# Seven block products for eight in the second layer's output projection of a hybrid decoder trunk

## The chip, the core and the metric

The kernel runs on one core of a Trainium2 chip. Its time is device microseconds of one execution; where several executions stand together, the median is given with the lowest and the highest. A profile is one execution of its own, recorded by the hardware. In it PE is TensorE (PEld its weight loads), DVE is VectorE, ACT is ScalarE, POOL is GpSimd, and SP is the engine that only issues transfers; SPq, ACTq and so on are what an engine's queue does beside its arithmetic, such as issuing a DMA. "L508" is line 508 of the profiled kernel.

## What is computed

Two decoder layers over 1024 tokens of width 1024 in float32. The reference, cut to what matters here:

```python
def hybrid_layer(x, c_act, ...):
    shift, scale, gate = split(c_act @ w_mod + b_mod, 3)
    h = rms_norm(x, pre_gain) * (1.0 + scale) + shift
    proj = h @ w_in                      # columns of three head groups and their gates
    a_out = sliding_window_attention(aq, ak, av, sinks) * silu(ag)      # 512 columns
    r_out = rms_norm(retention(rq, rk, rv)) * silu(rg)                  # 256 columns
    g_out = rms_norm(gated_linear_attention(...), gla_norm_gain) * silu(gg)  # 256 columns
    y = concatenate([a_out, r_out, g_out], axis=-1) @ w_out             # 1024 x 1024 @ 1024 x 1024
    return x + gate * rms_norm(y, post_gain)
```

The change is in the next-to-last line, for the second layer: the product of the gated mix (1024 tokens by 1024) with w_out (1024 by 1024).

## The kernel before

**Precision.** TensorE multiplies in a reduced float32 form, so every float32 operand is kept as a pair: a rounded high part and the low rest (high part: a cast on ACT or DVE; low part: a subtraction on DVE or POOL). A product is three passes: high by high, low by high, high by low.

**Order of the work.** A planner writes the program. Long rows of matmuls are written out in place (`mult`, `accum`), and every 7 of them `pump` lets waiting jobs (generators such as `gate`, `finish`, the attention blocks) put in their next piece if a table of due times says so. TensorE executes in exactly this order; the other engines' orders come from a scheduler, each engine working through its own queue in order. The table `EN` names the engine of each small operation ("A", "V", "G" are ACT, DVE, POOL; "S" and "A" for a transfer name the queue that issues it). Small tiles come from rings: `t2` (128x512, 14 buffers), `st` (5, weight pieces as they arrive), `smx` (6, softmax tiles), `mx` (2, the mix of one token tile, high and low), `mm` (3 accumulators of 512 columns in PSUM), `aux` (5, PSUM).

**Before the output projection.** Each head group stores its gated output to memory as high and low parts (`mixS`): `head_norm_gate` (L1029, where the gate multiplies the normalised heads, and the cast and subtraction behind it) and `gate` (the attention part: the attention blocks' values go from PSUM to SBUF by an ACT copy of L147, to memory as `aoS`, and back, transposed to the mix's layout; L1518 multiplies them by the gate, and L149 and L1521 split them). The last attention values of the layer are multiplied in the midst of the output projection of tile 0 and tile 1.

**The output projection.** `load` brings w_out in four pieces of 256 columns, `o0` to `o3`, and splits them (L147, L508). For each of the eight token tiles `load_mix` reads high and low parts; `y_half` accumulates half of the 1024 columns in 24 matmuls of 512 columns (3 passes by 8 blocks of 128 rows), ACT squares it with a sum (L1285), DVE multiplies it by the gate row `modg` (L1286). `finish` makes the reciprocal root (L561, L562), reads the residual and adds (L1330), and writes. The last two tiles (6 and 7) are held in the arenas, and the second half of the last tile is computed by `y_last` as two quarters of 256 columns (24 matmuls each; L1295 to L1304), so that most of its norm is done before the last quarter. Both layers do this.

## Time and profile before

| | |
|---|---|
| median of 3 runs | 958.48 us (956.33 to 959.75) |
| profiled execution: its time | 954.65 us |
| its span in the profile | 952.9 us |
| mean granted clock of TensorE | 0.997 |
| busy: PE, PEld | 932.7, 770.1 us |
| busy: DVE, ACT, POOL | 637.4, 474.1, 222.6 us |
| output projection of layer 2, first matmul | 854.43 us after the span's start |
| last matmul ends about | 947.06 us |

How to read it: the profiled execution's time lies 1.75 us above its span (what is outside the span), and 3.83 us below the median of the runs. Sums are made against the profiled execution and then moved to the median. "Busy" is time in which an engine executes; a group of instructions is a row with line, engine, operation, output<-input, shape, count, then busy us, mean ns of one, and the idle time before with what ended it. A timeline row has start, length, engine, line, operation, count, and in brackets the idle time before it with its releaser.

### The profile page before, as it was taken

To read this page: it belongs to the slowest core of one execution; us is meant where nothing else is said; L and a number is where in the kernel's file an instruction comes from. 1 tells how busy PE (TensorE), PEld (TensorE's weight loads), DVE (VectorE), ACT (ScalarE), POOL (GpSimd) and SP (SyncE) were. 2 spreads that over 40 slices of the span, in tenths; PEclk is the share of its full clock that TensorE was granted. 3 is DMA by queue.
4 is the path that set the end of the run, shared out by engine and by line. 5 is a ranking of instruction groups with operands and counts; after the bars stand their busy time and mean duration, and the time that the engine had idled before them with its cause. 6 is when DMAs were issued, how large, how long until landed. Compare 5 with 4: busy or idle time off the path is not lost.

```text
span 952.9 us, 15951 instructions
## 1 busy us (share of the span) xinstructions
PE 932.7 (98%) x5645; PEld 770.1 (81%) x5645; DVE 637.4 (67%) x1372; ACT 474.1 (50%) x1157; POOL 222.6 (23%) x288
## 2 busy tenths in 40 slices
PE   5999999999999999999999999999999999999997
PEld 1799887888888787778889888888888887787886
DVE  6886857757786988654685584694677787862332
ACT  3786233554756666622455532443667576661111
POOL 3222000423231324510131110033133033540000
PEclk9999999999999999999999999999999999999999
DMA  9943523613362345787455261362133222555951
GB/s 320 323 135 122 161 84 122 196 49 115 107 200 80 100 133 189 226 253 256 171 169 175 92 187 32 101 187 67 56 101 111 94 82 81 166 177 177 308 200 66
DMA packets 124651, 142.26 MB, mean 149 GB/s; under 512 B 11566, under 2 KB 95384, under 8 KB 124572
## 3 DMA queue, kind: packets, MB, share of 16 engines
q1 hardware_dynamic: 114396, 127.43, 42.1%
q10 hardware_dynamic: 10176, 13.82, 4.2%
q8 instruction: 44, 0.72, 0.3%
q14 instruction: 35, 0.29, 0.1%
HBM read 104.51 MB, written 36.70 MB: 148 GB/s over the span
## 4 chain that ended last, share of the span: by engine, by line
PE 85%; DVE 3%; issue 2%; ACT 2%; POOL 0%; DMA 0%; DVEq 0%; SPq 0%; POOLq 0%; ACTq 0%
PE mm L171 67%; PE aux L171 14%; PE aux L186 4%; ACT smx L971 0%; DMA t<-tabS 0%; ACT L1026 0%; DVE t L856 0%; ACT L1025 0%; DVE t L1029 0%; DVE t L1027 0%; DVE t L157 0%; ACT mx L1160 0%; DVE smx L966 0%; DVE arena L508 0%; DVE arena L149 0%
## 5 line engine op out<-in xcount | busy, mean ns | idle before, releaser
L171 PE MATMUL mm<-arena,arena 128*128 128x512 f32 (+2 forms) x1512 | 309.6, 358 | 0.0
L171 PE MATMUL mm<-arena 128*128 128x512 f32 (+2 forms) x1392 | 285.8, 359 | 0.0
L171 PEld LDWEIGHTS mm<-arena,arena 128*128 128x128 f32 x1512 | 246.5, 189 | 40.1 <-issue 2.1
L171 PEld LDWEIGHTS mm<-arena 128*128 128x128 f32 x1392 | 228.9, 190 | 37.2 <-issue 1.2
L171 PE MATMUL mm<-arena,mx 128*128 128x512 f32 (+1 forms) x696 | 157.3, 384 | 0.0
L171 PEld LDWEIGHTS mm<-arena,mx 128*128 128x128 f32 x696 | 126.5, 188 | 26.1 <-issue 1.5
L508 POOL TENSOR_TENSOR arena<-st,arena 128x512 fp32r<-128x512 f32 x57 | 85.9, 1512 | 158.0 <-ACT arena L147 100.3
L147 ACT ACTIVATE t<-aux 128x512 f32<-128x512 f32 x64 | 37.1, 591 | 82.6 <-PE aux L186 39.6
L508 DVE TENSOR_TENSOR arena<-st,arena 128x512 fp32r<-128x512 f32 x63 | 63.0, 1014 | 6.9 <-ACT arena L147 3.5
L147 ACT ACTIVATE arena<-st 128x512 fp32r<-128x512 f32 x82 | 48.4, 623 | 31.1 <-PE mm L171 15.0
L1285 ACT ACTIVATE t<-mm 128x512 f32<-128x512 f32 x30 | 17.9, 598 | 91.0 <-PE mm L171 46.3
L971 ACT ACTIVATE smx<-smx,sm 128x129 f32<-128x129 f32 x128 | 50.1, 394 | 18.1 <-DVE sm L968 17.9
L975 POOL TENSOR_TENSOR smx<-smx,sm 128x512 f32<-128x512 f32 x32 | 35.2, 1099 | 82.5 <-DVE sm L974 78.7
L384 DVE SCALAR_TENSOR_TENSOR acc<-st,c_act,acc 128x512 f32<-128x512 f32 x60 | 45.6, 760 | 13.1 <-DMA st<-in_w_mod_dram 12.1
L562 POOL TENSOR_TENSOR sm<-sm,few 128x1 f32<-128x1 f32 x26 | 14.8, 570 | 150.3 <-DVE sm L561 147.6
L1286 DVE TENSOR_TENSOR t<-mm,modg 128x512 f32<-128x512 f32 x30 | 20.7, 689 | 42.4 <-ACT t L1285 42.4
L1330 DVE SCALAR_TENSOR_TENSOR t<-t,sm,t 128x512 f32<-128x512 f32 x32 | 25.5, 827 | 30.8 <-DMA t<-xs 15.7
L186 PE MATMUL aux<-c_ident,t 128*128 128x128 f32 x224 | 33.7, 274 | 4.1 <-DVE t L634 2.3
L186 PEld LDWEIGHTS aux<-c_ident,t 128*128 128x128 f32 x224 | 26.6, 140 | 10.5 <-DVE t L634 2.7
L966 DVE COPY_PREDICATED smx<-c_curmask,aux 128x256 f32<-128x256 int32 x64 | 25.5, 447 | 12.8 <-ACT smx L147 11.4
L370 POOL MEMSET acc<- 128x512 f32 x4 | 2.1, 529 | 130.2 <-PE aux L171 119.1
L851 DVE TENSOR_TENSOR t<-mm,sincos 128x128 f32<-128x128 f32 (+2 forms) x36 | 16.2, 450 | 23.7 <-ACT t L147 12.5
(223 smaller groups left out, 1340.5 us busy)
## 6 DMA issues: line engine op xcount, KB each, us to landing
st<-in_w_in_dram SPq DMA_DIRECT2D x96, 256.0 KB, 3.9
st<-in_w_mod_dram SPq DMA_DIRECT2D x64, 256.0 KB, 3.0
mixS<-t SPq DMA_DIRECT2D x64, 256.0 KB, 2.5
mx<-mixS SPq DMA_DIRECT2D x28, 512.0 KB, 5.2
st<-in_w_out_dram SPq DMA_DIRECT2D x32, 256.0 KB, 3.2
wm<-in_w_mod_dram SPq DMA_DIRECT2D x12, 512.0 KB, 4.7
t<-in_x_dram SPq DMA_DIRECT2D x24, 256.0 KB, 4.9
t<-tabS SPq DMA_DIRECT2D x16, 256.0 KB
```

Source lines behind the costliest of these rows:

```text
L147: A.activation(dst, src, AF.Copy)
L171: T.matmul(dst, lhsT, rhs, start=start, stop=stop)
L186: T.transpose(dst, src, idn)
L384: V.scalar_tensor_tensor(acc, wt, c_act[:, k:k + 1], acc, ALU.mult, ALU.add)
L508: i = (G if first == 0 and kc in LOG else V if first == 0 else eng(f"wlo{kc}")).tensor_tensor(wt[:, 1, 2 * kc:2 * kc + 2, 0:256], st, f(hi ...
L851: V.tensor_tensor(a4, s4, cs.unsqueeze(1).unsqueeze(1).to_broadcast((P, nh, 2, 32)), ALU.mult)
L966: V.copy_predicated(sv, curmask.unsqueeze(1).to_broadcast((P, 2, P)), pv[:, :, n // P - 1, :])
L971: A.activation(sm[:, h, :], sm[:, h, :], AF.Exp, bias=mx[:, h:h + 1], accum_out=sums[:, h:h + 1])
L975: eng("pn").tensor_tensor(sm[:, :, 0:128], sm[:, :, 0:128], rs.unsqueeze(2).to_broadcast((P, 4, P)), ALU.mult)
L1285: A.activation(yg, pm, AF.Square, accum_out=ss[:, nh:nh + 1])
L1286: V.tensor_tensor(yg, pm, modg[l][:, 512 * nh:512 * nh + 512], ALU.mult)
L1330: V.scalar_tensor_tensor(xt[j], yg[j], r, xt[j], ALU.mult, ALU.add)
```

## The change

In the second layer the mix of a pair of token tiles is taken as a block matrix of two by two (two tiles of 128 tokens by two halves of 512 rows), w_out as two by two blocks of 512 by 512. Pair 0 (tiles 0 and 1) is computed as before, in four accumulations of 24 matmuls (`y_std`), second columns first. For pairs 1 to 3 seven block products of 12 matmuls (`product`) and fifteen sums stand in place of eight block products: 84 matmuls of 512 columns per pair where there were 96. Several products accumulate onto a PSUM tile that already holds one (`more`), with a copy of its state taken in between.

Of the fifteen sums four are of weights. They are made once, during pair 0: `fetch_chunk` reads the four blocks of w_out again, sixteen transfers of 256 KB, into `st` and `smx` tiles; `combine` makes the sums on DVE; `put` casts on ACT and subtracts on DVE (`ct0`, `ct1`) or POOL (`ct2`, `ct3`). Four are of the mix, once per pair (`operands`: `cs1`, `cs2` on POOL, `cs3`, `cs4` on DVE, and a split of each of the seven operands). Seven are of results (`y_pair`), of which some are the accumulation in PSUM. The mix of pairs 1 to 3 is therefore stored once in float32 (`mixF`) and read once; the cast and the subtraction in `head_norm_gate` and `gate` fall away for these. `load_block` loads w_out by blocks in place of `load`. `y_last` goes in both layers: the last half is one of 512 columns. In the last pair one half of a tile's final sum is put off (`late`): ACT scales it, POOL adds, and SP writes it after the last root.

```diff
-    def mult(dst, lhsT, rhs, start, stop, cost=None):
-        T.matmul(dst, lhsT, rhs, start=start, stop=stop)
+    def mult(dst, lhsT, rhs, start, stop, cost=None, more=False):
+        T.matmul(dst, lhsT, rhs, start=start, stop=stop, skip_group_check=more)
...
+        if l == DEPTH - 1 and p:
+            dma("smh", mixF[2 * p:2 * p + 2, :, kt0:kt0 + 2, :].rearrange("t p k q -> p t k q"),
+                g1.rearrange("p (t k q) -> p t k q", t=2, k=2))
+        else:
...
-    def y_last(l, mixt, ss, yg):
-        s3 = small(3)
-        for u in range(2):
-            pm = mm()[:, 0:256]
...
+    def load_block(l, kh, nh):
+        b = blk(BLK[kh][nh])
+        for i in range(4):
+            st = stage()
+            dma("lw", st, w_rows(l, 4 * kh + i, nh))
+            hi, lo = b[:, 0, i, :], b[:, 1, i, :]
+            if kh and i >= 2:
+                gain = gncol[:, l:l + 1]
+                A.activation(hi, st, AF.Copy, scale=gain)
+                V.scalar_tensor_tensor(lo, st, gain, f(hi), ALU.mult, ALU.subtract)
+            else:
+                copy(f"whi{i}", hi, st)
+                eng(f"wlo{i}").tensor_tensor(lo, st, f(hi), ALU.subtract)
...
+    def wide():
+        return gp.tile([P, 4, 129], F32, tag="smx", name=nm("wide"), bufs=SMB).rearrange("p h n -> p (h n)")[:, 0:512]
+    def fetch_chunk(l, i):
+        tl = []
+        for kh, nh in ((0, 0), (0, 1), (1, 1), (1, 0)):
+            t_ = wide() if i % 2 else stage()
+            dma("lw", t_, w_rows(l, 4 * kh + i, nh))
+            tl.append(t_)
+        return tl
+    def put(k, hi, lo, src):
+        A.activation(hi, src, AF.Copy)
+        eng(k).tensor_tensor(lo, src, f(hi), ALU.subtract)
+    def combine(l, i, tl):
+        b11, b12, b22, b21 = tl
+        def less(dst, x, y):
+            if i >= 2:
+                V.scalar_tensor_tensor(dst, x, gncol[:, l:l + 1], y, ALU.mult, ALU.subtract)
+            else:
+                V.tensor_tensor(dst, x, y, ALU.subtract)
+        V.tensor_tensor(b11, b12, b11, ALU.subtract)
+        less(b12, b22, b12)
+        less(b22, b22, b11)
+        less(b21, b21, b22)
+        for n, t_ in ((1, b22), (0, b11), (2, b12)):
+            put(f"ct{n}", blk(n)[:, 0, i, :], blk(n)[:, 1, i, :], t_)
+        return b21
+    def combine_last(i, t_):
+        b = blk(BLK[0][1])
+        put("ct3", b[:, 0, i, :], b[:, 1, i, :], t_)
...
+    def operands(raw):
+        a11, a12, a21, a22 = raw
+        res = {}
+        def keep(name, hi, lo, src):
+            put(f"co{name}", hi, lo, src)
+            res[name] = (k4(hi), k4(lo))
+        for n, src, tag in (("1", a11, "kT0"), ("2", a12, "kT1")):
+            o = gp.tile([P, 1024], F32R, tag=tag, name=nm("op"), bufs=1)
+            keep(n, o[:, 0:512], o[:, 512:1024], src)
+        s1, s2 = wide(), wide()
+        eng("cs1").tensor_tensor(s1, a21, a22, ALU.add)
+        eng("cs2").tensor_tensor(s2, s1, a11, ALU.subtract)
+        eng("cs3").tensor_tensor(a21, a11, a21, ALU.subtract)
+        yield res
+        x = mix_tile().rearrange("p a k q -> p (a k q)")
+        keep("6", x[:, 0:512], x[:, 512:1024], s2)
+        keep("7", x[:, 1024:1536], x[:, 1536:2048], a21)
+        eng("cs4").tensor_tensor(a12, a12, s2, ALU.subtract)
+        x = mix_tile().rearrange("p a k q -> p (a k q)")
+        keep("5", x[:, 0:512], x[:, 512:1024], s1)
+        keep("4", x[:, 1024:1536], x[:, 1536:2048], a22)
+        hi, lo = [gp.tile([P, 512], F32R, tag="st", name=nm("op"), bufs=BST) for _ in range(2)]
+        keep("3", hi, lo, a12)
+        yield res
+    def product(dst, a, b, start):
+        q = 0
+        for x, y in PASSES:
+            for k in range(4):
+                mult(dst, a[x][:, k, :], b[:, y, k, :], start and q == 0, q == 11, None, not start)
+                q += 1
+                if q % 6 == 0:
+                    pump()
...
+    def y_pair(l, p, o, soon):
+        t0, t1_ = 2 * p, 2 * p + 1
+        last = p == NP_ - 1
+        a, b, c = mm(), mm(), mm()
+        g0, g1 = modg[l][:, 0:512], modg[l][:, 512:1024]
+        sA, sB = small(2), small(2)
+        product(a, o["1"], blk(BLK[0][0]), True)
+        c11 = wide()
+        A.activation(c11, a, AF.Copy)
+        product(b, o["2"], blk(BLK[1][0]), True)
+        V.tensor_tensor(c11, b, c11, ALU.add)
+        A.activation(b, c11, AF.Square, accum_out=sA[:, 0:1])
+        eng("cg").tensor_tensor(c11, c11, g0, ALU.mult)
+        soon(0)
+        product(a, o["6"], blk(1), False)
+        c21 = wide()
+        A.activation(c21, a, AF.Copy)
+        product(c, o["7"], blk(2), True)
+        m7 = t2()
+        A.activation(m7, c, AF.Copy)
+        soon(1)
+        product(a, o["5"], blk(0), False)
+        c22 = wide()
+        A.activation(c22, a, AF.Copy)
+        eng("cc").tensor_tensor(c22, c22, m7, ALU.add)
+        A.activation(m7, c22, AF.Square, accum_out=sB[:, 1:2])
+        eng("cg2").tensor_tensor(c22, c22, g1, ALU.mult)
+        soon(2)
+        product(c, o["4"], blk(BLK[0][1]), False)
+        V.tensor_tensor(c21, c, c21, ALU.add)
+        A.activation(c, c21, AF.Square, accum_out=sB[:, 0:1])
+        V.tensor_tensor(c21, c21, g0, ALU.mult)
+        job(finish(l, t1_, sB, [c21, c22], None, (0,) if last else ()))
+        pump()
+        soon(3)
+        c12 = t2()
+        b22 = blk(BLK[1][1])
+        if not last:
+            product(a, o["3"], b22, False)
+            A.activation(c12, a, AF.Square, accum_out=sA[:, 1:2])
+            V.tensor_tensor(c12, a, g1, ALU.mult)
+            job(finish(l, t0, sA, [c11, c12]))
+            pump()
+            return
         r = small(1)
+        V.tensor_scalar(r, sA[:, 0:1], 1.0 / D, EPS, ALU.mult, ALU.add)
+        product(a, o["3"], b22, False)
+        sq = A.activation(c12, a, AF.Square, accum_out=sA[:, 1:2])
+        q = V.scalar_tensor_tensor(r, sA[:, 1:2], 1.0 / D, r, ALU.mult, ALU.add)
+        root = G.tensor_tensor(r, r, mhalf[:, 0:1], ALU.pow)
+        with tc.issue_after(sq.ins), tc.issue_after(root.ins):
+            for x, y, r7, t, sl in late:
+                A.activation(y, y, AF.Copy, scale=r7)
+                G.tensor_tensor(x, y, x, ALU.add)
+        for x, y, r7, t, sl in late:
+            dma("lx", out[0, t * P:(t + 1) * P, sl], x)
         with tc.issue_after(q.ins):
+            V.tensor_tensor(c12, a, g1, ALU.mult)
+        job(finish(l, t0, sA, [c11, c12], r))
+        pump()
+    def last_output(l):
+        mx = [load_mix(l, t) for t in range(2)]
+        await_flag(("mod", l, 2))
+        chunk = {0: fetch_chunk(l, 0), 1: fetch_chunk(l, 1)}
+        raw = load_pair(l, 1)
+        ss = [small(2) for _ in range(2)]
+        yg = [[t2(), t2()] for _ in range(2)]
+        held = {}
+        for n, (nh, t) in enumerate(((1, 0), (1, 1), (0, 0), (0, 1))):
+            y_std(l, t, nh, mx[t], ss[t], yg[t][nh])
+            held[n] = combine(l, n, chunk.pop(n))
+            if n < 2:
+                chunk[n + 2] = fetch_chunk(l, n + 2)
+            if n == 1:
+                for i in range(2):
+                    combine_last(i, held.pop(i))
+            if nh == 0:
+                job(finish(l, t, ss[t], yg[t]))
+                pump()
+            if n == 2:
+                prep = operands(raw)
+                o = next(prep)
+        for i in (2, 3):
+            combine_last(i, held.pop(i))
+        next(prep)
+        nxt = {}
+        for p in range(1, NP_):
+            def soon(i, p=p):
+                if p + 1 < NP_:
+                    if i == 0:
+                        nxt["raw"] = load_pair(l, p + 1)
+                    elif i == 2:
+                        nxt["prep"] = operands(nxt["raw"])
+                        nxt["o"] = next(nxt["prep"])
+            y_pair(l, p, o, soon)
+            if p + 1 < NP_:
+                next(nxt["prep"])
+                o = nxt["o"]
...
+    late = []
+    def finish(l, t, ss, yg, r=None, side=()):
         r = rstd2(ss) if r is None else r
         xt = [t2(), t2()]
         for j in range(2):
             sl = slice(512 * j, 512 * j + 512)
             dma("lx", xt[j], x_in[0, t * P:(t + 1) * P, sl] if l == 0 else xs[t, :, sl])
-            V.scalar_tensor_tensor(xt[j], yg[j], r, xt[j], ALU.mult, ALU.add)
+            if j in side:
+                late.append((xt[j], yg[j], r, t, sl))
+                continue
+            else:
+                V.scalar_tensor_tensor(xt[j], yg[j], r, xt[j], ALU.mult, ALU.add)
             dma("sx", out[0, t * P:(t + 1) * P, sl] if l == DEPTH - 1 else xs[t, :, sl], xt[j])
...
+            whole = (4, 2 if hf == 0 else 0)[l == DEPTH - 1]
+            if whole < 4:
+                dma("sm0", mixF[4 * hf + whole:4 * hf + 4, :, k, :].rearrange("t p q -> p t q"),
+                    ao[:, whole * P:].rearrange("p (t q) -> p t q", q=P))
...
+        if l == DEPTH - 1:
+            last_output(l)
+            return
...
-            r = None
-            if t == NT - 1:
-                r = y_last(l, hold[t][0], hold[t][1], hold[t][2][1])
-            else:
-                y_half(l, t, 1, hold[t][0], hold[t][1], hold[t][2][1])
-            job(finish(l, t, hold[t][1], hold[t][2], r))
+            y_half(l, t, 1, hold[t][0], hold[t][1], hold[t][2][1])
+            job(finish(l, t, hold[t][1], hold[t][2]))
             pump()
...
+BLK = ((3, 4), (5, 6))```

**PE, the pairs.** In before the second layer's projection ends as a list of accumulations, each into an accumulator of its own (mm; arena holds the weights and the last tiles' mix):

```order
L171 MATMUL mm_9783<-arena_357,mx_9678 128x512 x24
L171 MATMUL mm_9828<-arena_357,arena_73 128x512 x24
L171 MATMUL mm_9858<-arena_357,arena_73 128x512 x24
L171 MATMUL mm_9885<-arena_357,arena_73 128x512 x24
L171 MATMUL mm_9926<-arena_357,arena_73 128x256 x24
L171 MATMUL mm_9955<-arena_357,arena_73 128x256 x24
```

In the change pair 1 (op and mx are operands, 9578, 9579 and 9580 the three accumulators), is:

```order
L171 MATMUL mm_9578<-arena_358,op_9498 128x512 x12
L171 MATMUL mm_9579<-arena_358,op_9501 128x512 x12
L171 MATMUL mm_9578<-arena_73,mx_9563 128x512 x12
L171 MATMUL mm_9580<-arena_73,mx_9563 128x512 x12
L171 MATMUL mm_9578<-arena_73,mx_9569 128x512 x12
L171 MATMUL mm_9580<-arena_358,mx_9569 128x512 x12
L171 MATMUL mm_9578<-arena_358,op_9574 128x512 x4
L171 MATMUL mm_9578<-arena_358,op_9575 128x512 x4
L171 MATMUL mm_9578<-arena_358,op_9574 128x512 x4
```

The first accumulator is used by four of the seven products, the third by two.

**ACT, around the copy of the last attention values.** In before (aux is their PSUM tile, the rows of L1285 are squares of half tiles, L160 the writes of tile 0):

```order
L1285 ACTIVATE t_1644_9316,sm_9315<-mm_9318 128x512
L1285 ACTIVATE t_1645_9317,sm_9315<-mm_9389 128x512
L147 ACTIVATE t_1670_9449<-aux_9440 128x512
L160 DMA out_dram<-t_1662_9421 128x512
L160 DMA out_dram<-t_1663_9422 128x512
L1285 ACTIVATE t_1666_9433,sm_9432<-mm_9435 128x512
```

In the change (L1412 squares of half tiles, L1326 casts of weight sums and operands, L1423 the copy of the first product):

```order
L1412 ACTIVATE t_1659_9303,sm_9299<-mm_9383 128x512
L1326 ACTIVATE arena_73<-wide_9422 128x512
L1326 ACTIVATE arena_73<-wide_9424 128x512
L1326 ACTIVATE op_9574<-t_1651_9292 128x512
L147 ACTIVATE t_1680_9449<-aux_9440 128x512
L1326 ACTIVATE arena_358<-wide_9426 128x512
L1326 ACTIVATE mx_9563<-wide_9505 128x512
L1412 ACTIVATE t_1656_9300,sm_9298<-mm_9432 128x512
L1326 ACTIVATE mx_9563<-t_1652_9294 128x512
L160 DMA out_dram<-t_1685_9490 128x512
L160 DMA out_dram<-t_1686_9491 128x512
...
L1423 ACTIVATE wide_9595<-mm_9578 128x512
```

Three casts, the last of an operand of pair 1, now stand between the second square and the copy of the attention values.

**POOL, during pair 0.** In before the last rows of POOL are the small roots alone. In the change (L1327 low parts of weight sums and of operand 3, L1379 and L1380 operand sums):

```order
L1327 TENSOR_TENSOR arena_73<-st_9377,arena_73 128x512
L1379 TENSOR_TENSOR wide_9504<-t_1652_9294,t_1653_9296 128x512
L1327 TENSOR_TENSOR arena_358<-st_9280,arena_358 128x512
L1327 TENSOR_TENSOR arena_358<-wide_9288,arena_358 128x512
L1327 TENSOR_TENSOR arena_358<-st_9381,arena_358 128x512
L1380 TENSOR_TENSOR wide_9505<-wide_9504,t_1650_9290 128x512
L1327 TENSOR_TENSOR arena_73<-wide_9422,arena_73 128x512
L1327 TENSOR_TENSOR op_9575<-t_1651_9292,op_9574 128x512
```

The sum of L1380 stands behind three low parts of weights that go to arena_358, where pair 0's second columns were read from.

More of the change, by code (lines that the diff above doesn't have):

```diff
@@ new lines, in combine_last, with load_pair @@
+    def combine_last(i, t_):
+        b = blk(BLK[0][1])
+        put("ct3", b[:, 0, i, :], b[:, 1, i, :], t_)
+    def load_pair(l, p):
+        res = []
+        for t in (2 * p, 2 * p + 1):
+            for k in range(4):
+                await_flag(("mix1", l, t, k))
+            for kt0 in (4, 6):
+                await_flag(("mix", l, t, kt0))
+        for t in (2 * p, 2 * p + 1):
+            for kh in range(2):
+                a = t2()
+                dma("lmix", a.rearrange("p (k q) -> p k q", k=4), mixF[t, :, 4 * kh:4 * kh + 4, :])
+                res.append(a)
+        return res
@@ new lines, in product, with y_std @@
+    def product(dst, a, b, start):
+        q = 0
+        for x, y in PASSES:
+            for k in range(4):
+                mult(dst, a[x][:, k, :], b[:, y, k, :], start and q == 0, q == 11, None, not start)
+                q += 1
+                if q % 6 == 0:
+                    pump()
+    def y_std(l, t, nh, mixt, ss, yg):
+        pm = mm()
+        q = 0
+        for x, y in PASSES:
+            for k in range(KT):
+                mult(pm, mixt[:, x, k, :], blk(BLK[k // 4][nh])[:, y, k % 4, :], q == 0, q == 23)
+                q += 1
+                if q % CHUNK == 0:
+                    pump()
+        A.activation(yg, pm, AF.Square, accum_out=ss[:, nh:nh + 1])
+        V.tensor_tensor(yg, pm, modg[l][:, 512 * nh:512 * nh + 512], ALU.mult)
@@ L1591 @@
 BEGIN = 7
-MIXP = (6, 7)
+BLK = ((3, 4), (5, 6))
 B1L = 1
```

67 lines of the change are left out of this document (33 added, 34 removed).

## The prediction

> **What bounds the kernel now.** I read the page's head and slices first, then a table of the last stages, then the chain of waits.
>
> ```profile
> span 952.9 us, 15951 instructions
> PE 932.7 (98%) x5645; PEld 770.1 (81%) x5645; DVE 637.4 (67%) x1372; ACT 474.1 (50%) x1157; POOL 222.6 (23%) x288
> PE   5999999999999999999999999999999999999997
> ```
>
> TensorE (PE) is busy in every slice but the first and the last. So work taken from another engine earns nothing by itself, and a matmul taken away earns its whole duration, provided that its successor's operands are there.
>
> The table by stretches of the last stages (columns: length, then busy time of PE, PEld, DVE, ACT, POOL with counts, granted clock, DMA share, GB/s):
>
> ```profile
> 854.00:881.00 27.00, 27.00 (x138) 20.94 (x137) 9.78 (x17) 5.35 (x12) 3.86 (x5) 1.00 0.54 172
> 881.00:900.00 19.00, 19.00 (x86) 15.72 (x85) 7.36 (x15) 2.06 (x6) 1.22 (x2) 1.00 0.90 282
> 900.00:920.00 20.00, 20.00 (x90) 16.57 (x89) 6.08 (x13) 3.17 (x9) 1.10 (x2) 1.00 0.87 310
> 941.00:953.00 12.00, 6.06 (x50) 5.81 (x48) 4.70 (x12) 1.64 (x6) 1.10 (x2) 0.88 0.23 87
> ```
>
> Until 941 PE is full at full clock; VectorE (DVE) works 9.78 of 27 us in the first stretch, where the new sums go. The chain of waits (start, us, what) confirms PE up to the last half tile:
>
> ```profile
> 871.27 70.05 PE mm L171 x308
> 941.32 0.02 issue
> 941.35 0.70 ACT t L1285 x2
> ```
>
> 70.05 / 308 = 0.2274 us for a matmul of 512 columns.
>
> **What the change takes away.** Pairs 1 to 3 have 84 matmuls in place of 96 each: 36 x 0.2274 = **-8.2 us**. The two split halves (last tile of each layer) become whole halves. Their present cost, from the squares that follow each accumulation:
>
> ```profile
> 935.97 0.60 ACT L1285 ACTIVATE t<-mm 128x512 f32<-128x512 f32 x1 [4.81 <-PE mm L171]
> 941.35 0.60 ACT L1285 ACTIVATE t<-mm 128x512 f32<-128x512 f32 x1 [4.69 <-PE mm L171]
> 944.28 0.39 ACT L1295 ACTIVATE t<-mm 128x256 f32<-128x256 f32 x1 [2.25 <-PE mm L171]
> 947.10 0.38 ACT L1295 ACTIVATE t<-mm 128x256 f32<-128x256 f32 x1 [2.34 <-DMA out_dram<-t]
> ```
>
> A half tile takes 941.35 - 935.97 = 5.38 us, the split one 947.10 - 941.35 = 5.75: about 0.3 us more (24 x 0.2274 = 5.46), twice: **-0.6 us**. The single store of the gated mix removes casts and subtractions of DVE and halves those transfers; all this lies beside a full PE, so I count it at nothing. The sixteen weight reads add 4.2 MB; the smaller mix reads of six tiles take 3 MB away. At 172 GB/s for a share of 0.54 the engines could move about 318 GB/s, 8.6 MB in the 27 us against 4.6 MB moved; I count nothing, and up to 3 us if a piece comes late.
>
> **What it adds: a crowd on DVE and POOL.** This is the term that decides. First, what the two cost each other. The groups of DVE and POOL by shape, and a timeline where both work from SBUF:
>
> ```profile
> L1027 DVE TENSOR_TENSOR t<-t,t 128x512 f32<-128x512 f32 x16 | 11.1, 692 | 29.3 <-ACT t L1026 26.1 <-issue 3.1
> L1029 DVE TENSOR_TENSOR t<-aux,t 128x512 f32<-128x512 f32 x16 | 10.9, 684 | 0.3
> L508 POOL TENSOR_TENSOR arena<-st,arena x57: 1256/1487/1846, 20.9 to 842.2; 128x512 fp32r<-128x512 f32 x57
> 269.92 2.38 DVE L508 TENSOR_TENSOR arena<-st,arena 128x512 fp32r<-128x512 f32 x2
> 270.03 3.39 POOL L508 TENSOR_TENSOR arena<-st,arena 128x512 fp32r<-128x512 f32 x2 [3.02 <-ACT arena L147]
> 272.48 0.97 DVE L939 COPY smx<-sink 128x4 f32<-128x4 f32 x1
> 273.63 0.16 DVE L939 COPY smx<-sink 128x4 f32<-128x4 f32 x1
> ```
>
> A DVE sum takes 0.69 us, whether its operands lie in SBUF or one in PSUM; POOL's takes 1.256 at its shortest. Together they do not overlap: POOL's two take 3.39, DVE's two 2.38 in place of 1.38, and a copy of four columns takes 0.97 while POOL works and 0.16 after it. So a POOL subtraction inside a DVE stretch costs DVE 3.39/2 - 0.69 = 1.0 us.
>
> [...]
>
> Now the stretch. Let T0 = 854.43 be the start of the stage's first matmul. The rows of before that carry the steps:
>
> ```profile
> 853.73 0.69 DVE L1518 SCALAR_TENSOR_TENSOR t<-t,t 128x512 f32<-128x512 f32 x1 [1.57 <-DMA t<-aoS]
> 854.43 3.79 PE L171 MATMUL mm<-arena,mx 128*128 128x512 f32 x16
> 870.67 0.60 PE L171 MATMUL aux<-t,vd 128*64 128x256 f32 x4
> 871.37 0.60 ACT L147 ACTIVATE t<-aux 128x512 f32<-128x512 f32 x1 [2.15 <-issue]
> 871.99 0.37 SPq L160 DMA_DIRECT2D aoS<-t  x1
> 873.90 1.45 DVE L1330 SCALAR_TENSOR_TENSOR t<-t,sm,t 128x512 f32<-128x512 f32 x2 [3.71 <-DMA t<-xs]
> 876.61 0.92 SPq L160 DMA_DIRECT2D t<-aoS  x2
> 879.35 1.51 DVE L1518 SCALAR_TENSOR_TENSOR t<-t,t 128x512 f32<-128x512 f32 x2 [1.87 <-DMA t<-aoS]
> 881.57 0.60 ACT L1285 ACTIVATE t<-mm 128x512 f32<-128x512 f32 x1 [4.81 <-PE mm L171]
> L147 ACT ACTIVATE arena<-st 128x512 fp32r<-128x512 f32 x82 | 48.4, 623 | 31.1 <-PE mm L171 15.0
> ```
>
> 1. From the gate at 853.73 (L1727 in the new file) to the operand sum of L1386, DVE has 23 sums from SBUF and 3 with PSUM: 26 x 0.69 = 17.9 us. That sum takes what POOL's L1380 made, and POOL has nine 512-wide operations from SBUF in the same stretch: 9 x 1.0 = 9.0. I take DVE as supplied throughout. It ends at 853.73 + 26.9 = 880.7.
> 2. ScalarE (ACT) has the cast of that sum (0.62) ahead of the copy of the last attention values, though PE has these ready near 871. The copy starts at 881.3, and not at 871.37: 10 us late.
> 3. In before the copy at 871.37 goes out to memory and back, and the gates run at 879.35, 8.0 us after it. Now: 889.3. Behind the two gates (1.5) on DVE stand the two last sums of tile 0 (1.45): 892.3.
> 4. ACT must issue tile 0's two writes after these sums, and behind them in its queue stand the square of pair 0's last half, two casts and the copy of the first product: 0.4 + 0.6 + 1.25 + 0.6, so 895.1.
> 5. PE's third product accumulates onto the first one's PSUM tile and waits for that copy. Without a wait it would start after the fourth half (881.5) and two products (24 x 0.2274 = 5.46): 887.0. **Stall: +8.1 us.** Its bounds are 0 (copy of step 2 before 873.2) and 10.4 (nine POOL operations at 1.26).
>
> **Later pairs.** A pair has 12 DVE and 7 POOL operations of this kind: 12 x 0.69 + 7 x 1.0 = 15.3 us of its 84 x 0.2274 = 19.1. Throughput suffices, but three copies of ACT in each pair have only the next product, 2.7 us less 0.6, before PE wants the tile back, and ACT's queue puts casts that wait for a sum ahead of them. One DVE operation and two of POOL in the way (0.69 + 2 x 1.0 = 2.7, of which 2.1 is hidden) cost 0.6; bounds 0 and 5 (nine such places); I take four places: **+2.4 us**.
>
> **Tail.**
>
> ```profile
> 947.84 0.55 POOL L1302 TENSOR_TENSOR sm<-sm,few 128x1 f32<-128x1 f32 x1 [4.20 <-DVE sm L1301]
> 948.43 1.41 DVE L1330 SCALAR_TENSOR_TENSOR t<-t,sm,t 128x512 f32<-128x512 f32 x2 [0.33 <-POOL sm L1302]
> 949.21 1.00 ACTq L160 DMA_DIRECT2D out_dram<-t  x2
> ```
>
> The last square is 512 wide in place of 256 (0.60 for 0.38: +0.2); POOL's late sum (L1468), placed behind the root, meets DVE's last two sums (+1.0); its write is a third issue (+0.3): **+1.5 us** (0.3 to 2).
>
> **Clock.** Where PE started after idling, the clock was not full:
>
> ```profile
> 20.00:40.00 20.00, 19.98 (x98) 12.51 (x99) 18.74 (x37) 12.61 (x33) 7.12 (x11) 0.91 1.04 383
> ```
>
> 0.09 x 20 = 1.8 us lost there. The stall may cost as much; no row shows a stop of this length inside the stage, so I take a third: **+0.5** (0 to 1.8). [...]
>
> **Sum:** -8.2 - 0.6 + 8.1 + 2.4 + 1.5 + 0.5 = +3.7 on the profiled execution's 954.65: 958.4. That execution lies 3.8 under the median of the runs shown (958.48), so 962.2 there; I say **962.0**.
>
> **The rivals** (on the median's scale).
>
> *The cover holds (0.19, faster).* If DVE isn't the limit, because the gaps of POOL's casts let most pairs run apart and the copy of step 2 goes before 873.2, there is no stall: -8.8 + 1.5 + 0 to 2.4, so 951.2 to 953.6. For it: DVE works only 9.78 of 27 us now. Against: steps 1 and 2 stand in the order of the queues.
>
> *Half a stall (0.20, no change).* A copy near 878 leaves a stall of about 5: -8.8 + 4.9 + 2.4 + 1.5 = 0, 958.5. For it: step 1 takes DVE as never overlapped with POOL, although three of its sums read PSUM.
>
> [...]
>
> *The products do not shorten PE* (each 12 matmuls as long as before per column, counted in PE's queue): nothing speaks for it, and I leave it out.
>
> **How the numbers follow.** The forecast's own case (0.45) runs from 959.5 to 964.5. Runs spread by 0.3%, so less than 2.9 us, 955.6 to 961.4, is no change: of the forecast's 0.45 I give 0.13 to no change and 0.32 to slower; the whole lock is slower; half a stall is 0.16 no change, 0.04 faster; the cover that holds is faster. Faster 0.23, no change 0.29, slower 0.48. The range, 953.0 to 967.0, leaves out the better half of the first rival and the end of the third.
>
> **What would show it.** In the profile after: PE busy less by some 8 us; a gap of PE of 6 to 9 us before the third product of pair 1, near 887; the copy of the last attention values near 881; POOL and DVE operations of 1.5 us and more in 854 to 881; POOL's late sum between the two last of DVE. I am wrong if that copy stands near 871 and PE runs through, or if the gap stands elsewhere.

## The result, and the profile after

The changed kernel takes 966.16 us (median of 4 runs, 965.32 to 967.63) against 958.93 us before (median of 4, 956.33 to 959.75): a ratio of 1.0082, with a 95% interval of 1.0058 to 1.0105. It is slower by 7.2 us. The forecast was slower at 962.0, in a range of 953.0 to 967.0: the side is right and the time lies in the range, near its upper end.

The profiled execution of the changed kernel (967.63 us, span 965.8) is the longest of its four runs, while that of before (954.65) is shorter than all four. The two spans differ by 12.9 us and the medians by 7.2. So the stage's parts below are read from the two traces, and the sum is held against the medians only roughly.

The page's head of the changed kernel:

```profile
span 965.8 us, 15915 instructions
PE 931.7 (96%) x5561; PEld 762.9 (79%) x5561; DVE 677.4 (70%) x1396; ACT 497.1 (51%) x1197; POOL 270.7 (28%) x320
```

PE works a microsecond less, not eight, and is busy for 96% of a longer span (behind the first large gap 24 matmuls are busy for 8.74 us, where run 10 below has 24 in 5.60). The table by stretches of the changed kernel (columns as in the prediction) shows where:

```profile
854.00:881.00 27.00, 27.00 (x139) 20.91 (x138) 22.19 (x28) 14.60 (x38) 15.62 (x13) 1.00 0.63 202
881.00:900.00 19.00, 10.21 (x31) 7.10 (x29) 14.28 (x19) 7.65 (x17) 8.60 (x7) 0.78 0.45 138
```

In 881 to 900 PE works 10.21 of 19 us, at a granted clock of 0.78. DVE, with 9.78 us in the first stretch before, has 22.19, and POOL 15.62 where it had 3.86. PE's timeline from the first matmul of the stage, in full where it waits:

```profile
855.47 3.33 PE L171 MATMUL mm<-arena,mx 128*128 128x512 f32 x14
...
872.91 9.59 PE L171 MATMUL mm<-arena,mx 128*128 128x512 f32 x41
885.55 8.74 PE L171 MATMUL mm<-arena,op 128*128 128x512 f32 x24 [3.05 <-DVE t L1413]
900.30 13.47 PE L171 MATMUL mm<-arena,mx 128*128 128x512 f32 x48 [6.01 <-ACT wide L1423]
913.61 8.32 PE L171 MATMUL mm<-arena,op 128*128 128x512 f32 x36
922.93 5.73 PE L171 MATMUL mm<-arena,mx 128*128 128x512 f32 x24 [1.00 <-ACT wide L1423]
929.57 5.74 PE L171 MATMUL mm<-arena,mx 128*128 128x512 f32 x24 [0.91 <-ACT wide L1431]
...
944.46 11.20 PE L171 MATMUL mm<-arena,mx 128*128 128x512 f32 x48 [1.00 <-ACT wide L1423]
955.50 2.88 PE L171 MATMUL mm<-arena,op 128*128 128x512 f32 x12
```

There are two large gaps, before the first product (3.05 us) and before the third (6.01). After each the matmuls are slow: 24 take 8.74 us and 48 take 13.47, where run 10 below has such groups, unhindered, in 5.60 and 11.04. That is 3.1 and 2.4 us lost to the clock, whose granted value is 0.50 from 885.50 to 890.40, 0.86 from there to 894.30, and 0.50 from 900.30 to 905.10. Three gaps of about 1 us follow in pairs 2 and 3. The stage from its first matmul to the end of the last lasts 958.38 - 855.47 = 102.9 us; before, 947.06 - 854.43 = 92.6. Of the 10.3 us between them, the removed matmuls and the unsplit last half make -8.2 and -0.4, the large gaps +9.1, the clock +5.6, the small gaps +2.9. Most of the remaining 1.3 comes, by my estimate, from the shown ends of matmul groups: in run 10 the shown end of a group (881.21 + 5.60) lies 0.17 us behind the start of the next (886.64), and I count each of the five gaps as that much longer than shown.

What holds DVE up is plain in the timelines of DVE and POOL of the changed kernel:

```profile
877.45 1.77 DVE L1381 TENSOR_TENSOR t<-t,t 128x512 f32<-128x512 f32 x1
879.15 1.77 DVE L1327 TENSOR_TENSOR arena<-st,arena 128x512 fp32r<-128x512 f32 x1
880.85 1.77 DVE L1338 TENSOR_TENSOR wide<-wide,wide 128x512 f32<-128x512 f32 x1
876.94 1.74 POOL L1327 TENSOR_TENSOR arena<-st,arena 128x512 fp32r<-128x512 f32 x1
878.64 1.74 POOL L1327 TENSOR_TENSOR arena<-wide,arena 128x512 fp32r<-128x512 f32 x1
```

Each engine completes one operation per 1.70 us, in turns; the same DVE sums take 0.68 us where POOL rests. The last attention values and what stands behind them, in the chain of waits and then in ACT's timeline of the changed kernel:

```profile
891.21 3.09 DMA t<-aoS
894.31 0.70 DVE t L1727
```

```profile
888.03 0.58 ACT L147 ACTIVATE t<-aux 128x512 f32<-128x512 f32 x1
896.92 1.02 ACTq L160 DMA_DIRECT2D out_dram<-t  x2
899.66 0.58 ACT L1423 ACTIVATE wide<-mm 128x512 f32<-128x512 f32 x1
```

The copy starts at 888.03, right behind the cast of the operand sum; the second of the two gates at 894.31, the writes' issue at 896.92, and the copy of the first product, for which the third waits, ends at 900.24. The chain has the forecast's steps, 4 to 7 us later, and one wait that the forecast did not have: the last sums of tile 0 stand 1.1 us more for their residual (`xs`, the last row below), whose read SP issues at 891.76, behind that of the attention values. Part of the delay was there at the start: DVE stood twice for a piece of weights that had not landed.

```profile
853.65 0.69 DVE L1336 TENSOR_TENSOR st<-st,st 128x512 f32<-128x512 f32 x1 [3.02 <-DMA st<-in_w_out_dram]
858.99 1.44 DVE L1727 SCALAR_TENSOR_TENSOR t<-t,t 128x512 f32<-128x512 f32 x2 [1.57 <-DMA t<-aoS]
864.63 0.69 DVE L1336 TENSOR_TENSOR wide<-wide,wide 128x512 f32<-128x512 f32 x1 [2.08 <-DMA wide<-in_w_out_dram]
896.14 1.41 DVE L1539 SCALAR_TENSOR_TENSOR t<-t,sm,t 128x512 f32<-128x512 f32 x2 [1.13 <-DMA t<-xs]
```

### The profile page after: what moved, and what is told of

Same layout as the page of the kernel before. It is cut to its first block, busy times and chain, and to the rows that moved or that the text cites. A ratio compares the mean times of both kernels' runs of the same rounds, so it can differ in the third digit from the quotient of the medians.

```text
span 965.8 us, 15915 instructions
## 1 busy us (share of the span) xinstructions
PE 931.7 (96%) x5561; PEld 762.9 (79%) x5561; DVE 677.4 (70%) x1396; ACT 497.1 (51%) x1197; POOL 270.7 (28%) x320
## 4 chain that ended last, share of the span: by engine, by line
PE 79%; issue 4%; POOL 3%; DVE 3%; ACT 3%; DMA 1%; DVEq 0%; SPq 0%; ACTq 0%; POOLq 0%
PE mm L171 61%; PE aux L171 14%; PE aux L186 4%; POOL arena L1327 1%; POOL op L1327 0%; POOL mx L1327 0%; POOL wide L1439 0%; DMA mixF<-t 0%; DMA t<-aoS 0%; ACT smx L972 0%; DMA t<-tabS 0%; DVE t L1539 0%; POOL wide L1441 0%; ACT L1027 0%; POOL t L987 0%
## 5 line engine op out<-in xcount | busy, mean ns | idle before, releaser
L171 PE MATMUL mm<-arena,arena 128*128 128x512 f32 (+2 forms) x1392 | 287.6, 359 | 0.0
L171 PE MATMUL mm<-arena 128*128 128x512 f32 (+2 forms) x1392 | 284.6, 358 | 0.2 <-ACT arena L709 0.2
L171 PEld LDWEIGHTS mm<-arena 128*128 128x128 f32 x1392 | 227.3, 189 | 37.7 <-issue 1.2
L171 PEld LDWEIGHTS mm<-arena,arena 128*128 128x128 f32 x1392 | 227.2, 189 | 37.4 <-issue 2.1
L171 PE MATMUL mm<-arena,mx 128*128 128x512 f32 x624 | 149.6, 397 | 8.9 <-ACT wide L1423 8.0
L171 PEld LDWEIGHTS mm<-arena,mx 128*128 128x128 f32 x624 | 117.3, 191 | 36.1 <-ACT wide L1423 9.3
L509 POOL TENSOR_TENSOR arena<-st,arena 128x512 fp32r<-128x512 f32 x53 | 79.8, 1513 | 156.2 <-ACT arena L147 89.6
L147 ACT ACTIVATE t<-aux 128x512 f32<-128x512 f32 x64 | 36.8, 590 | 74.7 <-PE aux L171 36.1
L147 ACT ACTIVATE arena<-st 128x512 fp32r<-128x512 f32 x82 | 48.4, 624 | 30.3 <-PE mm L171 19.6
L509 DVE TENSOR_TENSOR arena<-st,arena 128x512 fp32r<-128x512 f32 x55 | 52.9, 976 | 7.1 <-ACT arena L147 4.0
L563 POOL TENSOR_TENSOR sm<-sm,few 128x1 f32<-128x1 f32 x27 | 15.7, 582 | 82.9 <-DVE sm L562 81.8
L852 DVE TENSOR_TENSOR t<-mm,sincos 128x128 f32<-128x128 f32 (+2 forms) x36 | 16.1, 449 | 22.2 <-ACT t L147 12.6
L655 ACT ACTIVATE t<-aux,mod,mod 128x128 f32<-128x128 f32 x56 | 21.2, 455 | 20.2 <-PE aux L186 11.8
L1028 DVE TENSOR_TENSOR t<-t,t 128x512 f32<-128x512 f32 x16 | 11.0, 690 | 29.3 <-ACT t L1027 26.2
L171 PE MATMUL mm<-arena,op 128*128 128x512 f32 x108 | 28.2, 420 | 3.1 <-DVE t L1413 3.0
```

The source lines that it names most:

```text
L147: A.activation(dst, src, AF.Copy)
L171: T.matmul(dst, lhsT, rhs, start=start, stop=stop, skip_group_check=more)
L509: i = (G if first == 0 and kc in LOG else V if first == 0 else eng(f"wlo{kc}")).tensor_tensor(wt[:, 1, 2 * kc:2 * kc + 2, 0:256], st, f(hi ...
L563: after[2] = G.tensor_tensor(r, r, mhalf[:, :w], ALU.pow)
L655: A.activation(hf[:, ks], pt[:, ks], AF.Identity, scale=gain, bias=shift)
L852: V.tensor_tensor(a4, s4, cs.unsqueeze(1).unsqueeze(1).to_broadcast((P, nh, 2, 32)), ALU.mult)
```

## The experiments

Each kernel was timed against the kernel before, which stood at 958.0 to 958.2 us in these comparisons.

**1. The tail alone.** `finish(..., (0,) if last else ())` became `finish(..., ())`.

> The changed kernel, but the last pair's put-off sum goes back to DVE (no scaling by ACT, no sum of POOL after the last root). Port theory: POOL's 1.39 us at the end stood between DVE's last two sums, so the time from the last matmul's end to the end of the span falls from 7.4 us to about 6.4 and the whole from 966.2 to about 965.2; everything before the tail stays, gaps of PE of 3.05 and 6.01 us included. Rival, the put-off sum was hidden beside the root: no change, 966.2, or up to 0.7 slower for one more sum of DVE.

Measured: 965.47 us (ratio 1.0075, 1.0054 to 1.0096), not to be told from the changed kernel, and between the two expectations; the trace decides. Without the put-off sum DVE has two sums before the last root and not one:

```profile
957.46 1.42 DVE L1539 SCALAR_TENSOR_TENSOR t<-wide,sm,t 128x512 f32<-128x512 f32 x2 [0.60 <-POOL sm L563]
958.79 0.15 DVE L1463 SCALAR_TENSOR_TENSOR sm<-sm,sm 128x1 f32<-128x1 f32 x1
```

From the last matmul's end (956.97) to the end of the span are 7.7 us, against 7.4 in the changed kernel. POOL's sum does stretch DVE's last sum there, to 1.75 us (the row below, of the changed kernel), but it also spares DVE one of 0.67 ahead of the root. The port theory's 1 us was wrong; the rival held.

```profile
960.83 1.39 POOL L1468 TENSOR_TENSOR t<-wide,t 128x512 f32<-128x512 f32 x1 [0.52 <-ACT wide L1467]
961.01 1.75 DVE L1539 SCALAR_TENSOR_TENSOR t<-t,sm,t 128x512 f32<-128x512 f32 x1
```

Up to its last pair this kernel is the changed one, and PE's timeline of this run shows that the large gaps have no fixed place:

```profile
884.43 3.01 PE L171 MATMUL mm<-arena,op 128*128 128x512 f32 x12 [1.36 <-DVE t L1413]
889.94 4.61 PE L171 MATMUL mm<-arena,op 128*128 128x512 f32 x12 [2.50 <-DVE t L1413]
898.79 13.58 PE L171 MATMUL mm<-arena,mx 128*128 128x512 f32 x48 [4.23 <-ACT wide L1423]
```

The first product runs at full speed (run 10: 12 matmuls in 2.88 us), and PE then waits 2.50 us for the second accumulator. In the profiled execution of the changed kernel the slow first product covers that wait.

**2. The copy of the last attention values first.** `pv[0]` is that copy.

```diff
+    def put(k, hi, lo, src, behind=False):
+        if behind:
+            with tc.issue_after(pv[0].ins):
+                A.activation(hi, src, AF.Copy)
...
```

`behind` holds for the last two of the four weight chunks and for operands 3 to 7.

> The changed kernel, with the copy of the last attention values placed on ACT ahead of the casts of the third and fourth weight chunk and of the operand sums, so that it goes near 874 and not at 888. Rival, queue order alone (the copy was late only because a cast stood before it): the gates run near 881, both gaps of PE before the third product (3.05 and 6.01 us) close, and with them the 5 to 6 us of slower clock: 953 to 956. Crowd theory (DVE's own queue is full until about 890, whoever is copied when): the gates still wait in DVE's queue until 888 or later, the gap before the third product falls from 6.0 to 4 or 5 us, the whole to 963 to 965.

Measured: 964.08 us (1.006, 1.004 to 1.008). ACT's and PE's timeline of this run:

```profile
872.36 0.60 ACT L1004 ACTIVATE t<-aux 128x512 f32<-128x512 f32 x1 [2.78 <-PE aux L171]
894.80 13.18 PE L171 MATMUL mm<-arena,mx 128*128 128x512 f32 x48 [7.07 <-ACT wide L1429]
```

The copy goes nearly 16 us earlier, and PE still waits 7.07 us, in one gap where there were 9.06 in two. The time is as the crowd theory had it, though not the gap, which it put at 4 to 5 us. DVE, which does not pause from 862.05 to 889.2, comes to the first gate at 885.15 and to the second at 891.97, and waits at neither for its input. So the cast ahead of the copy, which the prediction's step 2 named, was a place on the way and not the cause.

**3. POOL's share on DVE.**

```diff
-EN = {... "ct2": "G", "ct3": "G", ... "co5": "G", "co4": "G", "co3": "G", "cs1": "G", "cs2": "G", ...}
+EN = {... "ct2": "V", "ct3": "V", ... "co5": "V", "co4": "V", "co3": "V", "cs1": "V", "cs2": "V", ...}
```

> The changed kernel, with POOL's subtractions and sums of this stage (the low parts of two weight sums, two operand sums, three operand low parts) on DVE instead; POOL keeps two result sums a pair. Port theory: nine operations of POOL cost DVE 1.0 us each in the stretch of pair 0 and cost 0.69 on DVE itself, and no queue waits for the other any more: the sum of L1386 comes 3 to 5 us earlier, the gaps of PE before the third product (9 us in all) fall to 2 to 5, the whole to 956 to 961. Rival, plain load (POOL worked beside DVE for nothing): DVE has 9 x 0.69 = 6.2 us more before the third product, the gaps grow to 15 us, the whole to 972 or more.

Measured: 955.84 us (10 runs; 0.998, 0.9968 to 0.9992), 10.3 us under the changed kernel and 2.2 under the kernel before. More work on the busier engine makes the stage shorter, so plain load is out. The price fits the exclusion: while POOL worked beside it, one of its operations cost DVE about 1.0 us (1.70 less 0.69); on DVE itself it takes 0.6 (in this run such operations start at 874.20, 874.80 and 875.40). The move could also have taken away waits for POOL's results, but there were none to take: in the changed kernel's stage neither PE nor ACT nor DVE waited for one of the moved operations (DVE's 5.2 us of waiting for POOL are for the small root of L563). The scheduler may order the queues anew when an operation changes its engine; runs 9 and 10, where the orders that matter are fixed, answer that. PE's timeline:

```profile
891.25 5.76 PE L171 MATMUL mm<-arena,mx 128*128 128x512 f32 x24 [2.83 <-ACT wide L1423]
899.21 7.38 PE L171 MATMUL mm<-arena,mx 128*128 128x512 f32 x24 [2.20 <-ACT wide L1431]
...
914.58 11.08 PE L171 MATMUL mm<-arena,mx 128*128 128x512 f32 x48
```

The gap before the first product is gone, and so are those of pairs 2 and 3.

**4. Without the low parts of the summed weights.** In `put` for the weight sums the subtraction became a second cast by ACT, so the low parts are replaced by the high parts: eight operations each of DVE and POOL less, sixteen of ACT more.

> The changed kernel without the sixteen subtractions that make the low parts of the summed weights: ACT casts the sum a second time into their place, so the products with summed weights use the high part twice and not the low part. Crowd theory: DVE has 8 x 0.69 and POOL 8 x 1.0, 13.5 us, less in the stretch of pair 0, so the gates run by 881, both large gaps of PE (3.05 and 6.01) shrink to 0 to 3 us together, clock included: 953 to 957, what stays being the gaps of 1 us in later pairs. Rival, late weight transfers (DVE stood 3.0 and 2.1 us waiting for a chunk of weights): the transfers are as before, the gaps stay above 6 us, 961 to 966.

Measured: 959.85 us (10 runs; 1.0018, 1.0008 to 1.0028), between both expectations. The gaps fell from 12.0 us to 7.2 in all, not to 0 to 3. Thirteen of the sixteen added casts stood in ACT's queue ahead of the copy of the attention values, which still came only at 882.17:

```profile
882.17 0.57 ACT L147 ACTIVATE t<-aux 128x512 f32<-128x512 f32 x1
```

The run took work from two queues and put some into a third that was waited for as well, so it does not price the crowd cleanly: about five of the twelve microseconds went with the subtractions, and the rest can't be given to one cause by it.

**5. The writes of pair 0 behind the copy of the first product.** This takes out the prediction's step 4.

```diff
-        A.activation(c11, a, AF.Copy)
+        first = A.activation(c11, a, AF.Copy)
+        with tc.issue_after(first.ins):
+            while writes:
+                dma("sx", *writes.pop(0))
...
+            if l == DEPTH - 1 and t < 2:
+                writes.append((out[0, t * P:(t + 1) * P, sl], xt[j]))
```

> The changed kernel (POOL's share kept), but ACT issues pair 0's four writes of the output behind its copy of the first product of pair 1, not ahead of it. Chain theory (the third product waits for ACT's copy, the copy for the issue of tile 0's writes, these for DVE's last sums behind the late gates): without the issues ahead of it the copy ends near 893, before the second product's end at 894.3, and the gap of 6.01 us before the third product falls below 1.5; the gap of 3.05 before the first stays; since the gates are as late as before, 2 to 4 us come back before the fifth product or in pair 2, whose operands wait for the same gates; the whole 960 to 963.5. Rival, the copy is late for another reason (DVE or the sums themselves): 965 to 967.

Measured: 966.21 us (1.0088, 1.0073 to 1.0103): nothing gained. PE's timeline, and ACT's row behind the copy:

```profile
889.86 3.03 PE L171 MATMUL mm<-arena,op 128*128 128x512 f32 x12 [2.50 <-DVE t L1413]
...
896.64 3.06 PE L171 MATMUL mm<-arena,mx 128*128 128x512 f32 x12 [1.02 <-DVE t L1413]
903.34 7.08 PE L171 MATMUL mm<-arena,mx 128*128 128x512 f32 x24 [3.65 <-ACT wide L1434]
895.35 5.01 ACTq L160 DMA_DIRECT2D out_dram<-t  x4
```

The gap before the third product is gone, as the chain theory had it (1.11 us stay before the first). The 2.50 before the second product stands in run 1 as well; what is new are the gaps before the fourth and the fifth, 4.67 us for run 1's 4.23 before the third. All gaps together are 11.2 us, against 12.0. The four issues, which wait for DVE's last sums, now hold ACT ahead of its copy for the fifth product (L1434). So the edit moved the wait on to the next copy and did not take it away.

**6 to 8. Orders, with POOL's share on DVE.** Run 6 adds the writes behind the copy; run 7 adds run 2's order and this, which puts the last gates ahead of the operand sums; run 8 is run 7 with all writes of the output on SP's queue, in place of run 6's edit.

```diff
+        clk[0] += AHEAD
+        pump()
+        clk[0] -= AHEAD
         for i in (2, 3):
             combine_last(i, held.pop(i))
         next(prep)
```

> All of this stage's POOL subtractions and operand sums on DVE, as in the run before, and also pair 0's writes issued behind the copy of the first product. There the copy stood at 890.6 behind issues at 887.9 to 888.9 and the gap before the third product was 2.83. Chain theory: the copy goes by 887, that gap is 0; the gap of 2.20 before the fifth product and the clock behind it (1.9) stay or halve: 951.5 to 954. Rival, no more to gain there (the gates' lateness sets the pair): 955 to 957.

> As the run with all of it on DVE and the writes behind the copy, and also the copy of the last attention values ahead of ACT's casts and the last gates ahead of the operand sums in the program. Chain theory: the gates run near 884, the operands of pair 2 are stored and read back in time, and the gap before the fifth product falls below 1 us too, the clock stays full: 950 to 952.5, some 6.5 us under the kernel before, whose bound is the 8.8 us of matmuls less 1.5 for the tail. Rival, the stage is now short of DVE itself: gaps of 3 us or more stay, 953 to 956.

> As the run with gates first, but all writes of the output go through SP's queue and none through ACT's. Chain theory: ACT's queue is free of waits for DVE in all pairs, so the gaps are as small or smaller, 950 to 952.5 before the tail; at the end SP issues the last writes one after the other, up to 0.8 us later. Rival: SP's loads of the next pair's operands stand behind writes that wait for DVE, and gaps of 1 us a pair come back: 953 to 955.

Measured: 955.87 us (0.9969, 0.9954 to 0.9983), 954.32 (0.9962, 0.9947 to 0.9977) and 953.09 (0.995, 0.9933 to 0.9966). The chain theory's numbers were missed three times, and the rivals' fit in time. Run 6 gains nothing on run 3 (955.87 against 955.84), and the gaps of 1 us a pair that run 8's rival forecast are not in its trace. In all three the gap before the third product closed and one of 3 to 3.6 us stayed before the fifth. Run 8's timelines of PE and ACT name it:

```profile
896.57 5.73 PE L171 MATMUL mm<-arena,mx 128*128 128x512 f32 x24 [2.96 <-ACT wide L1437]
894.13 1.29 ACT L1332 ACTIVATE op<-t 128x512 fp32r<-128x512 f32 x2 [8.22 <-DMA t<-mixF]
```

ACT stands 8.22 us in front of the casts of pair 2's first operands, whose transfer comes after the gates; the copy that PE waits for is behind them. So what run 7's rival gave as a lack of DVE was, by then, the order of ACT's queue; run 10, where that order is changed, has no such gap.

**9 to 11. All orders put right, with POOL and without.** Beyond run 8: the casts of the next pair's first operands stand behind the copy of the fifth product, the square of the first result half behind that of the third, and the last pair's writes are again ACT's.

```diff
-        A.activation(b, c11, AF.Square, accum_out=sA[:, 0:1])
-        eng("cg").tensor_tensor(c11, c11, g0, ALU.mult)
         soon(0)
         product(a, o["6"], blk(1), False)
         c21 = wide()
-        A.activation(c21, a, AF.Copy)
+        third = A.activation(c21, a, AF.Copy)
+        with tc.issue_after(third.ins):
+            A.activation(b, c11, AF.Square, accum_out=sA[:, 0:1])
+        eng("cg").tensor_tensor(c11, c11, g0, ALU.mult)
...
-        A.activation(c22, a, AF.Copy)
+        fifth[0] = A.activation(c22, a, AF.Copy)
...
+                if fifth[0] is not None:
+                    es.enter_context(tc.issue_after(fifth[0].ins))
```

> The changed kernel with POOL's share kept, and every order that has stood in the way put right: the copy of the last attention values ahead of ACT's casts, the gates ahead of the operand sums, the writes of tiles 0 to 5 on SP, the square of the first result half behind ACT's copy for the fifth product, the casts of the next pair behind the copy of the fifth. Crowd theory (DVE and POOL exclude each other and have too little room, in pair 0 and later): gaps of 1 to 3 us come back in every pair, 8 to 10 us in all, the whole 959 to 963. Rival, queue orders alone: without the waits all 8.8 us of matmuls count, 950 to 952, the same as the next run.

> The same orders, with POOL's subtractions and operand sums on DVE. Both theories: no gap over 1 us in any pair, the clock full from the first product on; from the first matmul of the stage to the last 92.6 - 8.2 - 0.3 = 84.1 us, up to 86, and a tail of 7.4 as in the changed kernel, so 7 us under the kernel before less up to 1 for gaps: 950 to 952.5.

> The run just before without the put-off sum (all four last sums on DVE). From the run on the tail alone, where the tail took 7.75 us and not less: the put-off sum is worth nothing or 0.3 us; so the same as the run before within 1 us, 950 to 953. Port theory in its first form: 1 us faster at the end.

Measured: 963.67 us with POOL's share (6 runs; 1.0058, 1.0045 to 1.0072), 950.07 without (5 runs; 0.9911, 0.9897 to 0.9924), 949.17 without the put-off sum as well (4 runs; 0.9903, 0.989 to 0.9916; the last two can't be told apart). Run 9 lies just above the crowd theory's 959 to 963, with 9.0 us of gaps where it had 8 to 10; run 10 is as forecast, and run 11 is 0.8 us below its range. PE's timeline with POOL:

```profile
887.75 4.63 PE L171 MATMUL mm<-arena,op 128*128 128x512 f32 x12 [3.26 <-DVE t L1424]
911.77 4.61 PE L171 MATMUL mm<-arena,op 128*128 128x512 f32 x12 [2.49 <-ACT mm L1457]
936.02 4.61 PE L171 MATMUL mm<-arena,op 128*128 128x512 f32 x12 [2.48 <-ACT mm L1457]
```

and with everything on DVE:

```profile
854.33 3.33 PE L171 MATMUL mm<-arena,mx 128*128 128x512 f32 x14
...
881.21 5.60 PE L171 MATMUL mm<-arena,op 128*128 128x512 f32 x24
886.64 11.04 PE L171 MATMUL mm<-arena,mx 128*128 128x512 f32 x48
897.52 8.56 PE L171 MATMUL mm<-arena,op 128*128 128x512 f32 x36
...
936.04 2.88 PE L171 MATMUL mm<-arena,op 128*128 128x512 f32 x12
```

No gap is left; the stage lasts 938.92 - 854.33 = 84.6 us, the 84.1 that the forecast's terms give within half a microsecond. The four corners tell the causes apart: with POOL's share 966.16 by the old orders and 963.67 by the new ones, without it 955.84 and 950.07. The orders alone are worth 2.5 us, POOL's share alone 10.3, both 16.1, so 3.3 come only when both go. The first wait for weights stands in run 3 as well (2.59 us of DVE), where PE has no gap before the first two products, so that wait by itself, the larger part of run 4's rival, does not make the first gap. The seven products do save what they promise; the kernel of run 11 is 8.9 us under the kernel before (949.17 against 958.09 in its comparison).

## Why the prediction was right, and where it was off

**The gain.** 36 matmuls, -8.2 us: right, shown by the stage of run 10. The split halves, -0.3 each: layer 1's can be read from the two traces, of PE on both sides of its last half. Before:

```profile
475.60 11.15 PE L171 MATMUL mm<-arena,mx 128*128 128x512 f32 x48
500.45 10.10 PE L171 MATMUL mm<-arena,arena 128*128 128x272 f32 x79
```

and the changed kernel:

```profile
478.06 11.15 PE L171 MATMUL mm<-arena,mx 128*128 128x512 f32 x48
502.63 10.04 PE L171 MATMUL mm<-arena,arena 128*128 128x272 f32 x79
```

The changed kernel is 2.46 us behind on the first row (in that execution the clock in the first two stretches of 20 us was 0.94 and 0.89, in the one of before 1.00 and 0.91) and 2.18 on the next: 0.28 us gained, as forecast. Layer 2's lies inside the stage and can't be read by itself.

**The crowd (steps 1 to 5, +8.1).** The mechanism was right, its size too small. The third product starts 44.8 us after the stage's first matmul (900.30 - 855.47), in run 10 after 32.3 (886.64 - 854.33): 12.5 us late, where I had 8.1 and a bound of 10.4. (In run 1's execution it is 10.4.) That bound lets each operation of POOL cost DVE 1.26 us, all of POOL's own time; no run shows such a price, and the turns of 1.70 us make it 1.0. Of the signs that I named, the late copy (888.03 for 881), the long operations of DVE and POOL and a gap of 6 us before the third product are there; but 3.05 us of the gaps stand before the first product, where I had none. PE's first product needs an accumulator that DVE's multiplication by the gate row (L1413, at 884.82, behind chunk 3's sums) sets free, and I looked only at what the third product waits for.

The step that was mis-sized is step 1. It took DVE as supplied from 853.7; its gate ran at 858.99, behind 3.0 us of waiting for weights, with 2.1 us more later. That was the transfers that I counted at nothing, with up to 3 us if a piece came late: two did. The crowd's own price was near: 26.9 us forecast from the gate to L1386's end, 28.5 measured (858.99 to 887.46), of which 2.1 are the second wait for weights. Step 3 erred the other way and hid some of this: from the copy to the gates I had 8.0 us, and it took 5.6 (888.03 to 893.59). Step 2 named the cast ahead of the copy, and step 4 the writes' issue; runs 2 and 5 took each of these away and gained 2 us and nothing. So steps 2 to 4 describe the route of the delay, and the cause is step 1's crowd (runs 3, 9 and 10).

**The clock (+0.5).** This term was mis-sized too: 5.6 us are lost in the profiled execution, where my bound was 1.8. I had one stall and took a third of the 1.8 us of the program's start; there were two stalls, and 3.1 and 2.4 us were lost behind them. But the 3.1 behind the first gap cost nothing of their own: the third product waits for ACT's copy, which stands behind the writes' issue at 896.92, and a faster second product would only have waited longer (in run 1 the first product was fast, and the time went into a wait of 2.50). So what the clock adds to the stall is the 2.4.

**Later pairs (+2.4):** 2.9 in the trace, in three gaps, and 3.4 by comparison with run 10 (958.38 - 913.61 = 44.8 us, there 938.92 - 897.52 = 41.4). Run 3 shows that these too came from POOL's operations, since they vanish with them.

**Tail (+1.5):** 7.42 - 5.84 = 1.6 us, right in sum, but not as I divided it: POOL's put-off sum, to which I gave 1.0, costs nothing by run 1. What is left I read from DVE's rows and have not tested: the last product follows its neighbour by 2.7 us, so that one tile's sums still stand on DVE when the last square comes.

**The sum.** The two spans differ by 12.9 us where I had 3.7. Of the 9.2 between, the stall has 4.4, the clock 1.9, the later pairs 1.0, the slow start of that execution 1.3 (by T0, where 0.3 less was forecast and 1.0 more measured), the tail 0.1, and 0.5 are what run 10's stage, too, is longer than the forecast's terms. The medians differ by 7.2, about twice the forecast's 3.5: the profiled execution of before is 4.3 us under its median and that of the change 1.5 above. How the terms divide in the other executions is not known. That the time lies inside the range is in part luck: its upper part rests on the upper bounds, a stall of 10.4 and 1.8 of clock, and the profiled execution, at 12.5 and 2.4, goes beyond both.

**The rivals.** "The cover holds" was wrong for this kernel, and is what run 10 is: the same products, with a DVE that has room, at 950 us; I had 951.2 to 953.6 for it. "Half a stall" was wrong. Stall and clock both at their upper bounds give nearly the right time, 962.2 + 2.3 + 1.3 = 965.8, and not for the stall's reason: a pair of operations takes 1.70 us, as the forecast's 1.0 for POOL's share has it, and the stall grew by late weights instead.

## What to carry to other kernels

Before moving small operations onto the idle one of two engines, ask whether the two can work at once: here a DVE operation with its operands in SBUF and one of POOL took turns, a pair in 1.70 us where DVE's alone took 0.68, and 23 operations moved from POOL onto the busier DVE made the kernel 10 us faster. When the bound engine waits, remove the cause and not the place: two edits at the waits themselves gave 2 us and none, because the wait moved on to the next place. And count what a stall does to the clock as well as its length: here the matmuls behind the third product's gap lost 2.4 us. Clock lost ahead of a wait that another engine sets, like the 3.1 us behind the first gap, adds nothing to it.
